# Splitting the attention stage's weight blocks in two halves of 512 columns

## The chip, the core and the metric

The kernel runs on one core of a Trainium2 chip. The metric is the device time of one execution in microseconds (us). TensorE (PE in the profile) multiplies; VectorE (DVE), ScalarE (ACT) and GpSimd (POOL) do elementwise work; SyncE (SP) issues almost all DMA transfers. Each engine works through its own queue in order and waits on semaphores for the others.

## The reference, cut to what matters

One layer of a diffusion backbone, for 1024 latent tokens and 128 context tokens (1152 in all, nine tiles of 128), with a model width of 1024, all in float32:

```
h = rmsnorm(x, g1) * (1 + sc1) + sh1
u_f, q, k, v, g = split(h @ w_in)          # 512 + 1024 + 256 + 256 + 2048 columns
attn_o = attention(rope(q), rope(k), v)    # 16 query heads, 4 kv heads, window +-128, sink
m = sigmoid(g_f) * (fourier_mix(u_f) @ w_fo) + sigmoid(g_a) * (attn_o @ w_ao)
x = x + ga1 * (m @ w_out)
x = x + ga2 * (relu(h2 @ w_ff1) ** 2 @ w_ff2)
y = rmsnorm(x, final_g)
```

The change touches how the columns of `w_in` that make `q` (1024 columns) and the gate logits `g` (2048 columns) are prepared while the attention runs.

## The kernel before, in words

A float32 product is computed as three products of reduced-precision parts. Each operand is split into a high part, `hi = cast(x)` to the type F32R, and a low part, `lo = x - hi`; then `hi*hi + hi*lo + lo*hi` is summed in PSUM (`mm3`, lines 192 to 195). The cast is made on ACT, the subtraction on DVE (`sub`, line 140).

A weight block comes in as 128 partitions x 1024 columns of float32. `load_w` (line 152) takes a raw buffer `wraw` (two of them, shared by every weight load of this stage), issues the load on SP, and calls `split` (line 142), which takes one of three `whi` and one of three `wlo` buffers, casts the whole block on ACT (line 145) and subtracts the whole block on DVE (line 140). The raw buffer is free for the next load when the subtraction has read it.

The attention stage (lines 887 to 925) runs over 36 units: 4 kv groups x 9 token tiles. In a step of the loop, the program emits, in this order: the q projection of the next unit (`attention_q`: 24 matmuls, rotary on DVE, four transposes); the scores of this unit (`attention_scores`: matmuls at L705 and L706, mask and row maximum on DVE at L707, exponentials on ACT at L719, scaling on POOL at L729); the output of the unit before (`attention_out`: transposes at L748, cast `ph` on ACT at L753, subtraction `pl` on DVE, matmuls at L758 and L759, and `ot`/`at` at L762 to L765); and one filler. A filler (`filler`, line 488) is a third of a gate block: 24 matmuls (`gemm_unit`) whose result goes to DRAM. The first filler of a gate block also calls `load_w`. Of the 48 fillers 32 are emitted in this loop, and with them the weight blocks of gates 6 to 15: ten blocks of 8 x 128 columns.

The q weights come in per kv group: `load_q` (line 654) loads two blocks of 4 x 256 columns, k tiles 0 to 3 and 4 to 7, through the same raw buffers, casts each whole (line 662) and subtracts each whole. There are two `qwh` and two `qwl` buffers, so a group's q weights can be written only when the last q projection of the group before has read them. That makes eight blocks. Beside all this, ACT and POOL accumulate a modulation product (L303, L305), with a little DVE work at its end (L321, L322).

The order of the instructions in each engine's queue isn't the order of the program text. The kernel is built with `schedule_with_timeline_sim=True`: a planner simulates the engines, and when an engine comes free it takes, of what is ready in its simulation, what the program emitted first. The queues are then fixed. On the chip an instruction that is late holds up all that stands behind it on its engine.

Of the kernel before, what the change touches and what calls it, by code (L numbers as in the profile page):

```python
# [58 lines left out]
def backbone_kernel(  # L59
# [26 lines left out]
    nc = tc.nc  # L86
    uid = [0]

    def nm(s):
        uid[0] += 1  # L90
        return f"{s}_{uid[0]}"
# [47 lines left out]
    def sub(eng, dst, raw, hi):  # L139
        eng.tensor_tensor(dst, raw, hi.bitcast(F32), ALU.subtract)  # L140

    def split(raw, shape, lo_eng=None):
        hi = wp.tile(shape, F32R, tag="whi", name=nm("whi"), bufs=3)
        lo = wp.tile(shape, F32R, tag="wlo", name=nm("wlo"), bufs=3)
        nc.scalar.copy(hi, raw)  # L145
        sub(lo_eng or nc.vector, lo, raw, hi)
        return hi, lo

    def raw_w(shape):
        return wp.tile(shape, F32, tag="wraw", name=nm("wraw"), bufs=2)  # L150

    def load_w(src, r0, nk, c0, ncol):
        raw = raw_w([P, nk, ncol])
        nc.sync.dma_start(raw, src[r0 * P : (r0 + nk) * P, c0 : c0 + ncol].rearrange("(k p) n -> p k n", p=P))
        return split(raw, [P, nk, ncol])
# [181 lines left out]
    with ExitStack() as sf:  # L337
# [150 lines left out]
        def filler(n, after=None):  # L488
            for _ in range(n):
                if gates:  # L490
                    if after is None:
                        gates.pop(0)()
                    else:
                        with tc.issue_after(after):
                            gates.pop(0)()
# [5 lines left out]
        for o in range(0, NDFT, 1024):  # L501
            n = min(1024, NDFT - o)
            raw = raw_w([P, n])
# [81 lines left out]
    with ExitStack() as s1x:  # L585
# [68 lines left out]
        def load_q(g):  # L654
            out = []
            for hf in range(2):
                raw = raw_w([P, 4, 256])
                c0 = OFF_Q + g * 256
                nc.sync.dma_start(raw, w_in[hf * 512 : (hf + 1) * 512, c0 : c0 + 256].rearrange("(k p) n -> p k n", p=P))
                hi = p1.tile([P, 4, 256], F32R, tag="qwh", name=nm("qwh"), bufs=2)  # L660
                lo = p1.tile([P, 4, 256], F32R, tag="qwl", name=nm("qwl"), bufs=2)
                nc.scalar.copy(hi, raw)
                sub(nc.vector, lo, raw, hi)
                out.append((hi, lo))
            return out

        def attention_q(g, i, qw):
            psq = q1.tile([P, 512], F32, tag="q", name=nm("q"), bufs=1)
            r = slice(i * P, (i + 1) * P)
            for k in range(KC):  # L670
                wh, wl = qw[k // 4]
                mm3(psq[:, :256], h_hi[k][:, r], h_lo[k][:, r], wh[:, k % 4, :], wl[:, k % 4, :], k == 0, k == KC - 1)
            qsrc = psq[:, :256].rearrange("p (h d) -> p h d", h=4)
            qr = p1.tile([P, 4, HD], F32, tag="qr", name=nm("qr"), bufs=2)
            qhl = p1.tile([P, 4, 2, HD], F32R, tag="qhl", name=nm("qhl"), bufs=2)
            if i < 8:
                apply_rope(qr, qsrc, i, qhl[:, :, 0, :])
            else:
                nc.scalar.copy(qr, qsrc)
                nc.scalar.copy(qhl[:, :, 0, :], qsrc)  # L680
            sub(nc.vector, qhl[:, :, 1, :], qr, qhl[:, :, 0, :])
            psT = q1.tile([P, 512], F32R, tag="ptp", name=nm("ptp"), bufs=2)
            for h in range(4):
                ins = nc.tensor.transpose(
                    psT[:, h * P : (h + 1) * P], qhl[:, h].rearrange("p a d -> p (a d)"), identr
                )
            anchor = ins.ins
            qT = p1.tile([P, 4, P], F32R, tag="qT", name=nm("qT"), bufs=2)
            nc.scalar.copy(qT.rearrange("p h t -> p (h t)"), psT)  # L689
            return qT, anchor  # L690
# [80 lines left out]
        def load_kv(g):  # L771
            kd = p1.tile([P, 10, 2, HD], F32, tag="kd", name=nm("kd"), bufs=1)
            for e in range(2):
                nc.sync.dma_start(kd[:, :, e, :], kr_d[:, :, g, :])
            vg = p1.tile([P, 10, 2, HD], F32R, tag="vg", name=nm("vg"), bufs=2)
            nc.gpsimd.dma_start(vg, vh_d[:, :, g])
            return kd, vg

        def put_k(kd, q):
            pk = q1.tile([P, 512], F32, tag="ptp", name=nm("ptp"), bufs=2)  # L780
            for b in range(4):
                kb = {"c": 9, "x": 8}.get(KT_ORDER[q * 4 + b], KT_ORDER[q * 4 + b])
                nc.tensor.transpose(pk[:, b * P : (b + 1) * P], kd[:, kb].rearrange("p a d -> p (a d)"), ident)
            sl_ = slice(q * 512, (q + 1) * 512)
            nc.scalar.copy(kth[:, sl_], pk)
            sub(nc.vector, ktl[:, sl_], pk, kth[:, sl_])
# [5 lines left out]
        def load_fx():  # L792
            wfo.append(load_wfo(0))
            for i in range(4):
                raw = raw_w([P, FC])
                nc.sync.dma_start(raw, f_d[i])
                hi, lo = (slot(2 * i + e)[:, 0:FC] for e in range(2))
                nc.scalar.copy(hi, raw)
                sub(nc.vector, lo, raw, hi)
                fx.append((hi, lo))  # L800
            raw = raw_w([P, FC])
            nc.gpsimd.memset(raw, 0.0)
            for k in range(3):
                for r in range(2):
                    nc.sync.dma_start(raw[32 * k + 2 * r : 32 * k + 2 * r + 2], f_d[2 + r][0:65:64])
            ex, wex = fexw
            nc.scalar.copy(ex, raw[0:96])
            sub(nc.vector, ex[32:36], raw[32:36], ex[32:36])
            raw = raw_w([P, D])
            nc.gpsimd.memset(raw, 0.0)  # L810
            for k in range(3):
                nc.sync.dma_start(raw[32 * k : 32 * k + 4], w_fo.rearrange("(g c) n -> g c n", g=4)[:, 64])
            nc.scalar.copy(wex, raw[0:96])
            sub(nc.vector, wex[64:68], raw[64:68], wex[64:68])
# [69 lines left out]

        fbuf.append(fbuf_p1)

        units = [(g, i) for g in range(NG) for i in range(NTT)]
        kv = {0: load_kv(0)}
        qw = load_q(0)
        for q in range(3):  # L890
            put_k(kv[0][0], q)
        nxt = attention_q(0, 0, qw)
        pending = None
        for s, (g, i) in enumerate(units):
            qT, anchor = nxt
            if s + 1 < len(units):
                g1, i1 = units[s + 1]
                if i1 == 0:
                    qw = load_q(g1)
                nxt = attention_q(g1, i1, qw)  # L900
                anchor = nxt[1]
            pts = attention_scores(g, i, qT)
            if i == 0 and g:
                put_k(kv[g][0], 2)
            if g + 1 < NG:
                if i == 2:
                    kv[g + 1] = load_kv(g + 1)
                if i == 4:
                    put_k(kv[g + 1][0], 0)
                if i == 7:  # L910
                    put_k(kv[g + 1][0], 1)
            if pending is not None:
                attention_out(*pending)
                if s % SKIP:
                    filler(1, anchor)
            pending = (g, i, pts, kv[g][1])
            if s >= len(units) - 2:
                if s == len(units) - 2:
                    filler(100, anchor)
                    load_fx()  # L920
                f_unit(NF)
# [36 lines left out]
    with ExitStack() as sao:  # L958
# [18 lines left out]
        for m in range(KC):  # L977
            if m < 7:
                hi, lo = ER[:, 2 * m * NT : (2 * m + 1) * NT], ER[:, (2 * m + 1) * NT : (2 * m + 2) * NT]
            else:  # L980
                hi, lo = (p3.tile([P, NT], F32R, name=nm("at7")) for _ in range(2))
# [949 lines left out]
```

## Time and profile before

| | |
|---|---|
| time, median of 3 runs | 1698.27 us (1697.79 to 1698.74) |
| profiled execution, its own time | 1695.32 us |
| span of the profiled execution | 1693.5 us |
| PE busy, whole span | 97% |
| DVE, ACT, POOL busy, whole span | 70%, 53%, 18% |
| attention stage | about 228 to 690 us of the span |
| mean granted TensorE clock, whole span | 0.995 |

"Busy" is time in which an instruction of that engine was running. For PE it is time in which at least one matmul was in flight, so it is not the same as full speed. A window's row gives, for each engine, the busy us and the number of instructions, then the granted TensorE clock (1.00 is full speed), the busy share of the DMA engines and their rate. In rows of a timeline the first number is the start, the second the duration, both in us; the square bracket at the end tells how long the engine stood idle before the instruction, and what it waited for.

### The profile page before, as it was taken

The numbers are of one execution on the slowest core, as the hardware profiler recorded it, in microseconds if no ns is written. First come the engines' busy times: TensorE is split into PE (matmuls) and PEld (weight loads), VectorE is DVE, ScalarE is ACT, GpSimd is POOL, SyncE is SP. The second block draws the span as 40 slices with busy tenths as digits, with TensorE's granted clock in tenths as the row PEclk, the third lists the DMA queues.
The fourth block names the chain that finished last, engine by engine and source line by source line (L and its number), as shares of the span: only waits on it lengthen the run. The fifth ranks groups of instructions, "written<-read, shape, count | busy, mean of one in ns | idle before, by whom it ended". The sixth has DMA issues, their size and how long they took to land.

```text
span 1693.5 us, 26361 instructions
## 1 busy us (share of the span) xinstructions
PE 1635.2 (97%) x9053; PEld 1450.9 (86%) x9053; DVE 1184.4 (70%) x2408; ACT 903.8 (53%) x1826; POOL 297.5 (18%) x374
## 2 busy tenths in 40 slices
PE   6999999999999999899999899999999999999997
PEld 5799889999899999889988788888888888888886
DVE  7653247778777877778757876777776488776764
ACT  6443236766767767655436664444444454444542
POOL 3510004435444534400001500000000200000000
PEclk9999999999999999999999999999999999999999
DMA  8342391223322321279656434455446996656751
GB/s 298 114 133 70 128 256 51 77 76 80 90 75 79 94 59 51 78 245 313 197 183 202 156 107 152 159 168 168 161 151 152 307 381 205 199 190 195 244 167 62
DMA packets 204629, 265.56 MB, mean 157 GB/s; under 512 B 31992, under 2 KB 132280, under 8 KB 204496
## 3 DMA queue, kind: packets, MB, share of 16 engines
q1 hardware_dynamic: 196240, 253.92, 46.7%
q0 software_dynamic: 8256, 9.96, 2.3%
q8 instruction: 71, 1.16, 0.3%
q14 instruction: 62, 0.51, 0.1%
HBM read 195.38 MB, written 68.44 MB: 156 GB/s over the span
## 4 chain that ended last, share of the span: by engine, by line
PE 77%; DVE 8%; ACT 4%; issue 3%; DMA 2%; POOL 1%; SPq 0%; DVEq 0%; ACTq 0%; POOLq 0%
PE x L1674 6%; PE x L1675 6%; PE x L1673 6%; PE x L1277 6%; PE x L1279 6%; PE x L1278 6%; PE mm L193 3%; PE mm L194 3%; PE mm L195 3%; PE x L193 2%; PE x L194 2%; PE x L195 2%; PE ptp L748 2%; DVE pt L707 2%; PE o L759 1%
## 5 line engine op out<-in xcount | busy, mean ns | idle before, releaser
L140 DVE TENSOR_TENSOR wlo<-wraw,whi 128x1024 fp32r<-128x1024 f32 x100 | 125.8, 1260 | 80.7 <-ACT whi L145 80.5
L145 ACT CAST whi<-wraw 128x1024 fp32r<-128x1024 f32 x98 | 102.5, 1050 | 90.1 <-PE x L233 20.1
L1674 PE MATMUL x<-BR 128*128 128x512 f32 x336 | 130.7, 389 | 0.0
L1675 PE MATMUL x<-BR 128*128 128x512 f32 x336 | 130.2, 389 | 0.0
L1673 PE MATMUL x<-BR 128*128 128x512 f32 x336 | 129.0, 389 | 0.0
L729 POOL TENSOR_SCALAR pt<-pt,mx 128x512 f32<-128x512 f32 (+2 forms) x144 | 97.2, 687 | 158.1 <-DVE mx L727 141.8
L719 ACT ACTIVATE pt<-pt,mx 128x513 f32<-128x513 f32 (+2 forms) x144 | 94.7, 660 | 33.2 <-DVE mx L717 32.7
L707 DVE CUSTOM_DVE_ANT_0 pt<-s,mask,sink 128x512 f32<-128x512 f32 (+2 forms) x144 | 94.7, 673 | 20.4 <-PE ptp L748 11.3
L1646 ACT CAST BR<-aa 128x512 fp32r<-128x512 f32 x80 | 49.7, 621 | 103.5 <-PE x L1674 48.3
L140 DVE TENSOR_TENSOR pl<-ptp,ph 128x512 fp32r<-128x512 f32 (+1 forms) x136 | 86.0, 640 | 15.9 <-ACT ph L753 14.8
L305 POOL TENSOR_TENSOR macc<-macc,mprod 128x512 f32<-128x512 f32 x70 | 92.2, 1317 | 20.2 <-ACT mprod L303 20.1
L194 PE MATMUL mm<-BR,whi 128*128 128x384 f32 x272 | 91.9, 338 | 0.0
L753 ACT CAST ph<-ptp 128x512 fp32r<-128x512 f32 (+1 forms) x136 | 72.6, 546 | 31.7 <-PE ptp L748 30.3
L1277 PE MATMUL x<-BR,whi 128*128 128x512 f32 (+2 forms) x204 | 79.6, 390 | 4.1 <-ACT ZR L1301 2.8
L193 PE MATMUL mm<-BR,whi 128*128 128x384 f32 x240 | 83.5, 348 | 0.0
L195 PE MATMUL mm<-BR,wlo 128*128 128x384 f32 x240 | 81.2, 338 | 0.0
L748 PE MATMUL ptp<-ident,pt 128*128 128x128 f32 x496 | 76.5, 275 | 2.4 <-ACT qT L689 2.1
L1279 PE MATMUL x<-BR,wlo 128*128 128x512 f32 (+2 forms) x204 | 78.1, 383 | 0.0
L1278 PE MATMUL x<-BR,whi 128*128 128x512 f32 (+2 forms) x204 | 78.0, 382 | 0.0
L303 ACT ACTIVATE mprod<-mraw,siluc 128x256 f32<-128x256 f32 x140 | 63.8, 503 | 20.6 <-POOL macc L305 19.5
L140 DVE TENSOR_TENSOR BR<-aa,BR 128x512 fp32r<-128x512 f32 x80 | 55.0, 687 | 28.3 <-ACT BR L1646 27.7
L1673 PEld LDWEIGHTS x<-BR 128*128 128x128 f32 x336 | 63.1, 188 | 13.2
(462 smaller groups left out, 5199.8 us busy)
## 6 DMA issues: line engine op xcount, KB each, us to landing
aa<-hr_d SPq DMA_DIRECT2D x108, 256.0 KB
ab<-in_w_ff_dram SPq DMA_DIRECT2D x108, 256.0 KB
hr_d<-ZR SPq DMA_DIRECT2D x104, 256.0 KB
wraw<-in_w_in_dram SPq DMA_DIRECT2D x40, 512.0 KB
wraw<-in_w_ff_dram SPq DMA_DIRECT2D x34, 512.0 KB
mraw<-in_w_ada_dram SPq DMA_DIRECT2D x96, 128.0 KB
wraw<-in_w_out_dram SPq DMA_DIRECT2D x24, 512.0 KB
z_d<-z SPq DMA_DIRECT2D x48, 192.0 KB
```

The source lines that it names most:

```text
L140: eng.tensor_tensor(dst, raw, hi.bitcast(F32), ALU.subtract)
L193: nc.tensor.matmul(out, ah, bh, start=start, stop=False)
L194: nc.tensor.matmul(out, ah, bl, start=False, stop=False)
L195: return nc.tensor.matmul(out, al, bh, start=False, stop=stop).ins
L707: nc.vector.tensor_tensor_reduce(out=pt[:, e, :n], in0=sp[:, :n], in1=mask[:, m0 : m0 + n], scale=1.0, scalar=sink8[:, h0 + e : h0 + e + 1 ...
L748: nc.tensor.transpose(pst[:, bi, e, :], pt[:, e, b * P : (b + 1) * P], ident)
L1277: nc.tensor.matmul(po, wh, xh, start=(k == 0 and not cont), stop=False, skip_group_check=cont)
L1278: nc.tensor.matmul(po, wh, xl, start=False, stop=False, skip_group_check=cont)
L1279: nc.tensor.matmul(po, wl, xh, start=False, stop=(k == 3), skip_group_check=cont)
L1673: nc.tensor.matmul(ps, xh, bh, start=start, stop=False, skip_group_check=cont)
L1674: nc.tensor.matmul(ps, xh, bl, start=False, stop=False, skip_group_check=cont)
L1675: nc.tensor.matmul(ps, xl, bh, start=False, stop=stop, skip_group_check=cont)
```

## The change

`split` gets a switch, `parts`. With `parts[0] == 1` it does what it did. While `parts[0]` is 2, it casts and subtracts a block in two halves: cast of half 0, subtraction of half 0, cast of half 1, subtraction of half 1, as the program emits them. The switch is 2 from the start of the attention loop to its last step but one, so it holds for the ten gate blocks; `load_q` does the same for its eight blocks at all times. Each half is 512 columns. Buffers, loads, matmuls and numbers computed stay the same.

```diff
+    parts = [1]
+
     def split(raw, shape, lo_eng=None):
         hi = wp.tile(shape, F32R, tag="whi", name=nm("whi"), bufs=3)
         lo = wp.tile(shape, F32R, tag="wlo", name=nm("wlo"), bufs=3)
-        nc.scalar.copy(hi, raw)
-        sub(lo_eng or nc.vector, lo, raw, hi)
+        if parts[0] == 1:
+            nc.scalar.copy(hi, raw)
+            sub(lo_eng or nc.vector, lo, raw, hi)
+            return hi, lo
+        n = shape[1] // parts[0]
+        for i in range(parts[0]):
+            c = slice(i * n, (i + 1) * n)
+            nc.scalar.copy(hi[:, c], raw[:, c])
+            sub(nc.vector, lo[:, c], raw[:, c], hi[:, c])
         return hi, lo
...
                 hi = p1.tile([P, 4, 256], F32R, tag="qwh", name=nm("qwh"), bufs=2)
                 lo = p1.tile([P, 4, 256], F32R, tag="qwl", name=nm("qwl"), bufs=2)
-                nc.scalar.copy(hi, raw)
-                sub(nc.vector, lo, raw, hi)
+                for c in (slice(0, 2), slice(2, 4)):
+                    nc.scalar.copy(hi[:, c], raw[:, c])
+                    sub(nc.vector, lo[:, c], raw[:, c], hi[:, c])
                 out.append((hi, lo))
...
+        parts[0] = 2
         units = [(g, i) for g in range(NG) for i in range(NTT)]
         kv = {0: load_kv(0)}
         qw = load_q(0)
...
             if s >= len(units) - 2:
+                parts[0] = 1
                 if s == len(units) - 2:
                     filler(100, anchor)
                     load_fx()
```

## The prediction

> **What bounds the kernel now.** I read the page first: the busy shares and the chain of work that ended last.
>
> ```profile
> span 1693.5 us, 26361 instructions
> ...
> PE 1635.2 (97%) x9053; PEld 1450.9 (86%) x9053; DVE 1184.4 (70%) x2408; ACT 903.8 (53%) x1826; POOL 297.5 (18%) x374
> ...
> PE 77%; DVE 8%; ACT 4%; issue 3%; DMA 2%; POOL 1%; SPq 0%; DVEq 0%; ACTq 0%; POOLq 0%
> ```
>
> PE sets the time: busy for 97% of the span and 77% of the chain. So the change counts only where it alters PE's idle time or PE's clock. The profiled execution took 1695.32 us, 1.82 us more than its span; the median shown is 2.95 us above it. I work out a difference on the trace and put it on the median.
>
> Second, the busy time by window: the attention stage (228 to 690), then 3.41 us windows around each stretch in which the clock was halved, and one more window (692) for comparison.
>
> ```profile
> core 0: us, PE busy (x) PEld busy (x) DVE busy (x) ACT busy (x) POOL busy (x), PEclk, DMA share, GB/s
> 371.15:374.56 3.41, 1.62 (x10) 1.17 (x8) 2.86 (x6) 2.46 (x7) 0.55 (x2) 1.00 0.08 22
> 374.56:377.97 3.41, 3.41 (x16) 3.19 (x15) 2.23 (x8) 0.81 (x2) 0.00 (x0) 0.50 0.72 216
> 429.18:432.59 3.41, 1.88 (x12) 1.42 (x11) 3.17 (x10) 3.19 (x8) 1.63 (x3) 1.00 0.51 148
> 432.59:436.00 3.41, 3.41 (x15) 3.41 (x15) 3.08 (x6) 2.30 (x5) 0.00 (x0) 0.50 0.24 60
> 555.47:558.88 3.41, 1.72 (x13) 1.39 (x12) 3.41 (x8) 2.98 (x6) 1.05 (x2) 1.00 0.28 88
> 558.88:562.29 3.41, 3.41 (x13) 2.57 (x13) 3.41 (x8) 0.71 (x2) 0.93 (x2) 0.50 0.75 220
> 692.00:695.41 3.41, 1.77 (x13) 1.44 (x12) 1.71 (x5) 2.43 (x6) 1.59 (x4) 1.00 0.47 176
> ...
> 228.00:690.00 462.00, 443.03 (x3085) 424.79 (x3085) 347.22 (x937) 317.54 (x789) 200.25 (x276) 0.99 0.30 83
> ```
>
> In the stage PE is busy for 443.0 of 462 us, DVE for 75%, ACT for 69%. Three times the clock is granted at 0.50 for 3.41 us while PE is busy throughout; each time the window before had PE busy for half or less (1.62, 1.88, 1.72 us). Each stretch costs 3.41 x 0.5 = 1.7 us, the three 5.1 us. The window at 692 had 1.77 us and kept its clock, so the level near which it falls isn't sharp.
>
> Third, the waits of PE and of its weight loads over the stage (us in total, times, longest).
>
> ```profile
> PE s L705 <- DVE mx L707: 5.8, 8, 1.6
> PE o L759 <- DVE pl L140: 4.0, 3, 1.7
> PE ptp L684 <- DVE pl L140: 3.7, 4, 1.6
> ...
> PEld q L194 <- DVE qwl L140: 0.3, 1, 0.3
> ```
>
> PE waits for DVE's softmax and `pl` results, and but once, for 0.3 us, for a weight split. Splits hurt by standing in front of others, which the timeline shows at four places (DVE rows, then the PE row that waited).
>
> ```profile
> 330.28 1.23 DVE L140 TENSOR_TENSOR wlo<-wraw,whi 128x1024 fp32r<-128x1024 f32 x1 [0.71 <-ACT whi L145]
> 331.42 0.75 DVE L707 CUSTOM_DVE_ANT_0 pt<-s,mask,sink 128x512 f32<-128x512 f32 x1
> ...
> 332.23 0.50 PE L705 MATMUL s<-kth,qT 128*128 128x512 f32 x1 [1.06 <-DVE mx L707]
> ...
> 370.00 1.03 ACT L145 CAST whi<-wraw 128x1024 fp32r<-128x1024 f32 x1
> 371.05 0.26 ACT L762 COPY ot<-o 64x128 f32<-64x128 f32 x1
> ...
> 372.24 1.23 DVE L140 TENSOR_TENSOR wlo<-wraw,whi 128x1024 fp32r<-128x1024 f32 x1
> 373.50 0.62 DVE L707 CUSTOM_DVE_ANT_0 pt<-s,mask,sink 128x384 f32<-128x384 f32 x1
> ...
> 374.18 0.45 PE L705 MATMUL s<-kth,qT 128*128 128x384 f32 x1 [1.47 <-DVE mx L707]
> ...
> 428.17 1.23 DVE L140 TENSOR_TENSOR qwl<-wraw,qwh 128x1024 fp32r<-128x1024 f32 x1 [1.22 <-ACT qwh L662]
> ...
> 430.14 1.07 ACT L753 CAST ph<-ptp 128x512 fp32r<-128x512 f32 x2
> ...
> 431.63 1.28 DVE L140 TENSOR_TENSOR pl<-ptp,ph 128x512 fp32r<-128x512 f32 x2
> ...
> 432.37 0.42 PE L759 MATMUL o<-pl,vg 128*128 128x256 f32 x1 [0.95 <-DVE pl L140]
> ...
> 556.33 1.19 DVE L140 TENSOR_TENSOR wlo<-wraw,whi 128x1024 fp32r<-128x1024 f32 x1
> 557.43 0.41 DVE L322 TENSOR_REDUCE red<-mraw 128x8 f32<-128x256 f32 x1
> 557.75 0.68 DVE L140 TENSOR_TENSOR pl<-ptp,ph 128x512 fp32r<-128x512 f32 x1
> ...
> 558.49 0.39 PE L759 MATMUL o<-pl,vg 128*128 128x256 f32 x1 [1.69 <-DVE pl L140]
> ```
>
> At 330, 372 and 556 a 1.2 us subtraction runs directly or one short step ahead of what PE waits for; near 428 the subtraction is ahead of a queue of softmax work that ends in the wait at 432. Three of the four lie in the windows before a halved clock.
>
> **The change part by part.** Eighteen casts of 1024 columns become 36 of 512, and so the subtractions. No transfer, buffer or matmul changes.
>
> ```profile
> L1646 ACT CAST BR<-aa 128x512 fp32r<-128x512 f32 x80 | 49.7, 621 | 103.5 <-PE x L1674 48.3 <-issue 40.6 <-DMA aa<-hr_d 10.2
> L662 ACT CAST qwh<-wraw 128x1024 fp32r<-128x1024 f32 x8 | 8.4, 1054 | 2.2 <-DMA wraw<-in_w_in_dram 2.2
> L140 DVE TENSOR_TENSOR BR<-aa,BR 128x512 fp32r<-128x512 f32 x80 | 55.0, 687 | 28.3 <-ACT BR L1646 27.7
> ```
>
> *Added work.* A cast of 512 columns from SBUF takes 0.621 us elsewhere in this kernel, a subtraction 0.687 us. Where two halves are parted by other work, a block costs 2 x 0.621 - 1.054 = +0.19 us on ACT and 2 x 0.687 - 1.23 = +0.14 us on DVE. Where they follow each other, they overlap: the two `pl` at 431.63 took 1.28 us together, +0.05, and the two `ph` at 430.14 1.07 us, +0.02. For 18 blocks that is 1.3 us at least, 18 x 0.33 = 5.9 us at most, on both engines together. It is hidden by their idle time in the stage (115 us on DVE, 144 us on ACT); without that cover it would all be PE's loss. The bounds are 0 and +5.9; I take +1.0, the lower sum with most of it on the path, since PE's waits above are for DVE, and DVE's input there comes from ACT.
>
> [...]
>
> *Work let in between.* If the planner puts a waiting instruction between the halves, it starts 1.23 - 0.687 = 0.54 us sooner behind a subtraction, 1.05 - 0.62 = 0.43 us behind a cast (at 371.05 `ot` stands right behind a 1.03 us cast, and `at` on DVE behind it). At the four places that is 4 x 0.54 + 0.43 = 2.6 us at most. The order is fixed by simulated times, so the slot may go to an instruction that nobody waits for. I take half, -1.3; bounds -2.6 and 0.
>
> *The clock.* With 0.54 us more of PE work, the three windows would hold 2.2 to 2.4 us, above all three that led to a halved clock. I take two of three gone: -3.4; bounds -5.1 and, since a re-planned order can stall PE elsewhere, +3.4 (two new stretches).
>
> *An earlier first half.* The second q block of group 1 is read as soon as it is there:
>
> ```profile
> 334.38 1.18 DVE L140 TENSOR_TENSOR qwl<-wraw,qwh 128x1024 fp32r<-128x1024 f32 x1
> ...
> 335.62 0.39 PE L194 MATMUL q<-qwl,BR 128*128 128x256 f32 x1
> ```
>
> PE reads it 0.06 us after its end. Two of its four k tiles would be there 0.54 us sooner, but score matmuls fill most of that wait: 0 to -0.5, I take -0.3. For the other blocks the 0.3 us of direct waits above is the cap, so they earn nothing.
>
> *Sum:* +1.0 - 1.3 - 3.4 - 0.3 = -4.0 us. 1695.32 becomes 1691.3 for the profiled execution; on the median, 1698.27 - 4.0 = 1694.3 us.
>
> **The rivals.**
>
> *Nothing moves.* The planner sees both halves ready one behind the other and takes them so; the waiting work stays behind 1.28 us instead of 1.23. For it: a cast's second half needs only the raw block, which is already there. Against it: DVE gets the second half only when ACT has cast it, about half a microsecond after the first (half of the 1.07 us of the two `ph`), time enough for another instruction. The clock stretches stay, the overhead of about 1 us stays: 1699.3 us. [...]
>
> *Everything goes.* All three stretches and all of the waiting in front of splits vanish: +0.6 - 2.6 - 5.1 - 0.5 = -7.6, 1690.7 us. Against it: the planner doesn't know which stall costs a clock stretch.
>
> *Slower: a late second half at a group's head.* Once a subtraction is two instructions, other DVE work can come ahead of the second. At the head of group 1 there is no cover (0.06 us), and behind the q matmul in PE's in-order queue stand scores, outputs and fillers. An L707 (0.75) and a `pl` (0.68) between the halves hold PE for 1.4 us; with the clock stretch such a wait can bring that is 1.4 + 1.7 = 3.1 us. It decides from about one such wait with no relief elsewhere: 1.0 + 3.1 = +4.1, 1702.4 us. For it: DVE is at 75% and three engines hand work round. Against it: only one of the three later heads is that tight in the waits above.
>
> **How the numbers follow.** The forecast has 0.42, with a range of its own from 1691.5 to 1697; everything goes 0.12; nothing moves 0.27; slower 0.19. The limits of a difference that this measurement can tell are 0.2%, 3.4 us: 1694.9 and 1701.7. Of the forecast's chance 0.32 lies below 1694.9 and 0.10 within; all of "everything goes" is below; nothing moves gives 0.24 within and 0.03 above; the slower case 0.16 above and 0.03 within. That is 0.44 faster, 0.37 the same, 0.19 slower. The range reaches to 1688 (everything goes, and some other stalls with it) and to 1702.5 (the slower case).
>
> **What would show it.** Right: on DVE an L707, `pl` or `at` between two halves of 0.69 us; fewer than three windows at clock 0.50 between 228 and 690; PE's waits for L707 and `pl` shorter in sum than 13.5 us. Wrong: halves side by side at all 18 blocks; as many halved stretches, at other places; a PE wait for `qwl` of over 1 us; or a stage whose length changes while its clock stretches don't, which would put the gain or loss in the re-planned order and not in what I summed.

## The result and the profile after

| | before | after |
|---|---|---|
| time, median of 5 runs | 1697.79 us (1695.16 to 1698.74) | 1705.63 us (1704.57 to 1706.86) |
| ratio | | 1.0052, 95% interval 1.0039 to 1.0065 |
| profiled execution, its own time | 1695.32 us | 1704.57 us |
| span of the profiled execution | 1693.5 us | 1702.8 us |
| mean granted TensorE clock | 0.995 | 0.992 |

The change makes the kernel slower by 8.8 us by the ratio (7.8 us between the medians). Its 1705.63 us lie above the forecast of 1694.3 us and above the top of its range, 1702.5 us. The busy shares and the chain hardly show it. They answer the first lines of the prediction:

```profile
span 1702.8 us, 26393 instructions
...
PE 1640.8 (96%) x9053; PEld 1454.9 (85%) x9053; DVE 1187.8 (70%) x2426; ACT 905.8 (53%) x1844; POOL 293.7 (17%) x374
...
PE 76%; DVE 8%; ACT 4%; DMA 3%; issue 2%; POOL 1%; SPq 0%; DVEq 0%; ACTq 0%; POOLq 0%
```

VectorE has 18 instructions and 3.4 us more, TensorE the same 9053 and 5.6 us more. To find the place I took one event that each unit of the attention has once, ScalarE's cast of the transposed q (L689 before, L699 after), and compared its start in both traces. Up to unit 28 the two stay together: 617.31 us before, 618.83 after. At unit 33 they stand at 675.39 and 685.91. So of the 9.3 us by which the spans differ, 1.5 lie ahead of unit 28, nine arise between these two events, and 1.2 us are won back in the 1000 us behind them. The nine are no chance of one execution: in all runs below that keep before's order there, this step takes 58.06 to 58.10 us. Here is that stretch, by window: first from unit 28 to 29, then from 29 to 30, then the whole from 28 to 33. The columns are those of the prediction's windows. Before:

```profile
617.31:626.43 9.12, 9.12 (x63) 8.83 (x63) 7.92 (x21) 7.03 (x19) 4.06 (x6) 1.00 0.24 74
626.43:638.33 11.90, 9.91 (x71) 8.44 (x70) 10.64 (x32) 9.41 (x26) 7.51 (x11) 1.00 0.20 51
617.31:675.39 58.08, 56.09 (x389) 52.98 (x389) 47.78 (x133) 44.86 (x116) 28.17 (x39) 1.00 0.19 58
```

and after:

```profile
618.83:631.92 13.09, 11.17 (x78) 10.61 (x77) 11.89 (x37) 9.54 (x26) 6.37 (x9) 1.00 0.28 83
631.92:644.83 12.91, 11.06 (x66) 9.82 (x67) 11.04 (x28) 9.20 (x25) 8.04 (x11) 0.87 0.08 22
618.83:685.91 67.08, 60.50 (x394) 56.44 (x393) 49.99 (x141) 45.36 (x118) 29.97 (x41) 0.95 0.17 51
```

The whole stretch is 67.08 us instead of 58.08, nine more. TensorE stands idle for 67.08 - 60.50 = 6.6 us of it, where it was 58.08 - 56.09 = 2.0: 4.6 us of new waits. It is busy for 4.4 us longer, and the granted clock of 0.95 says why: two half-clock stretches lie in it, which cost 2 x 3.41 x 0.5 = 3.4 us. The last 1.0 us goes with the five more matmul records that fall into this window. The stretches show in aligned windows, each with the window ahead of it:

```profile
628.97:632.38 3.41, 1.48 (x13) 1.22 (x11) 3.33 (x13) 2.76 (x8) 1.13 (x3) 1.00 0.45 132
632.38:635.79 3.41, 3.41 (x12) 2.61 (x11) 3.35 (x7) 2.65 (x9) 2.16 (x3) 0.50 0.07 19
656.27:659.68 3.41, 1.54 (x11) 1.37 (x12) 2.90 (x10) 2.13 (x5) 2.32 (x3) 1.00 0.07 19
659.68:663.09 3.41, 3.41 (x13) 3.41 (x11) 1.91 (x6) 1.74 (x5) 1.33 (x2) 0.50 0.13 38
```

**No halved block is anywhere near.** The last one of the changed kernel is subtracted at 584 us; the one weight block of this stretch, at 624 us, is split whole in both kernels. What differs is the order. From 624 us in the changed kernel, on VectorE and on TensorE (start, duration, and in the bracket the idle time and what ended it):

```profile
624.43 1.35 DVE L140 TENSOR_TENSOR wlo<-wraw,whi 128x1024 fp32r<-128x1024 f32 x1 [0.97 <-PE mm L204]
...
629.54 0.46 PE L694 MATMUL ptp<-identr,qhl 128*128 128x128 f32 x4
631.94 1.31 PE L758 MATMUL ptp<-ident,pt 128*128 128x128 f32 x6 [1.94 <-DVE pl L140]
...
629.49 0.75 DVE L717 CUSTOM_DVE_ANT_0 pt<-s,mask,sink 128x512 f32<-128x512 f32 x1
630.17 0.75 DVE L717 CUSTOM_DVE_ANT_0 pt<-s,mask,sink 128x512 f32<-128x512 f32 x1
631.37 0.42 DVE L140 TENSOR_TENSOR pl<-ptp,ph 128x256 fp32r<-128x256 f32 x1
```

and the same transposes of unit 29 before:

```profile
625.40 0.46 PE L684 MATMUL ptp<-identr,qhl 128*128 128x128 f32 x4
...
626.35 0.28 PE L193 MATMUL q<-qwh,BT 128*128 128x256 f32 x1
...
627.77 0.28 PE L195 MATMUL q<-qwh,BR 128*128 128x256 f32 x1
627.89 0.82 PE L748 MATMUL ptp<-ident,pt 128*128 128x128 f32 x6
```

Before, ten matmuls of a q projection, which depend on nothing in the softmax, and four score matmuls stand between the transposes of q and the next transposes of probabilities. After, all 24 of that projection have been issued ahead, the `pl` that PE waits for stands on VectorE behind two softmax passes of 0.75 us, and PE waits 1.94 us. Whether the missing matmuls or the order on VectorE make this wait, these rows can't say.

The places that the prediction named look like this in the changed kernel:

```profile
330.20 0.69 DVE L140 TENSOR_TENSOR wlo<-wraw,whi 128x512 fp32r<-128x512 f32 x1
330.81 0.75 DVE L717 CUSTOM_DVE_ANT_0 pt<-s,mask,sink 128x512 f32<-128x512 f32 x1
...
332.15 1.34 DVE L140 TENSOR_TENSOR wlo<-wraw,whi 128x512 fp32r<-128x512 f32 x1
...
373.67 1.29 DVE L140 TENSOR_TENSOR wlo<-wraw,whi 128x512 fp32r<-128x512 f32 x2
...
375.67 0.44 PE L715 MATMUL s<-kth,qT 128*128 128x384 f32 x1 [1.54 <-DVE mx L717]
...
547.16 2.51 DVE L140 TENSOR_TENSOR qwl<-wraw,qwh 128x512 fp32r<-128x512 f32 x4
...
552.26 0.51 PE L694 MATMUL ptp<-identr,qhl 128*128 128x128 f32 x4 [2.39 <-DVE pl L140]
```

At 330 two softmax passes come between the halves as forecast, and the wait of 1.06 us there is gone. At 372 the halves lie side by side (1.29 us for both), and the wait is 1.54 us where it was 1.47. The wait at 556 has given way to a worse one at 552: two q blocks, four halves in a row, then 2.39 us. Over the stage, 228 to 700 us, PE's waits (us in total, times, longest):

```profile
PE ptp L694 <- DVE pl L140: 9.7, 9, 2.4
PE o L768 <- DVE at L775: 4.2, 4, 1.6
PE s L715 <- DVE mx L717: 3.0, 4, 1.5
PE ptp L758 <- DVE pl L140: 2.3, 2, 1.9
PE o L769 <- DVE pl L140: 2.1, 3, 0.9
```

Waits for the row maximum fell from 5.8 to 3.0 us; waits for `pl` rose from 4.0 + 3.7 to 9.7 + 2.3 + 2.1, and those for `at` from 1.3 to 4.2.

### The profile page after: what moved, and what is told of

Read it like the earlier page. It is cut to its first block, busy times and chain, and to the rows that moved or that the text cites. A ratio compares the mean times of both kernels' runs of the same rounds, so it can differ in the third digit from the quotient of the medians.

```text
span 1702.8 us, 26393 instructions
## 1 busy us (share of the span) xinstructions
PE 1640.8 (96%) x9053; PEld 1454.9 (85%) x9053; DVE 1187.8 (70%) x2426; ACT 905.8 (53%) x1844; POOL 293.7 (17%) x374
## 4 chain that ended last, share of the span: by engine, by line
PE 76%; DVE 8%; ACT 4%; DMA 3%; issue 2%; POOL 1%; SPq 0%; DVEq 0%; ACTq 0%; POOLq 0%
PE x L1686 6%; PE x L1687 6%; PE x L1685 6%; PE x L1289 6%; PE x L1291 6%; PE x L1290 6%; PE mm L202 3%; PE mm L203 3%; PE mm L204 3%; PE x L202 2%; PE x L203 2%; PE x L204 2%; PE ptp L758 2%; DVE pt L717 2%; PE x L240 1%
## 5 line engine op out<-in xcount | busy, mean ns | idle before, releaser
L140 DVE TENSOR_TENSOR wlo<-wraw,whi 128x1024 fp32r<-128x1024 f32 (+1 forms) x110 | 130.8, 1194 | 82.6 <-ACT whi L148 73.0
L148 ACT CAST whi<-wraw 128x1024 fp32r<-128x1024 f32 x88 | 92.1, 1051 | 84.4 <-PE x L242 21.8
L729 ACT ACTIVATE pt<-pt,mx 128x513 f32<-128x513 f32 (+2 forms) x144 | 94.8, 662 | 36.4 <-DVE mx L727 35.9
L1686 PEld LDWEIGHTS x<-BR 128*128 128x128 f32 x336 | 63.1, 188 | 13.1
L1685 PEld LDWEIGHTS x<-BR 128*128 128x128 f32 x336 | 63.0, 188 | 13.1
```

The source lines that it names most:

```text
L1685: nc.tensor.matmul(ps, xh, bh, start=start, stop=False, skip_group_check=cont)
L1686: nc.tensor.matmul(ps, xh, bl, start=False, stop=False, skip_group_check=cont)
```

## The experiments

The planner writes the order anew for every program. Set side by side in queue order, at least 581 TensorE, 218 VectorE, 119 ScalarE and 53 SyncE instructions stand elsewhere in the changed kernel. To part order from halves I fixed the order by hand: after the program is emitted, an order-only edge joins each instruction of a queue to the next, in an order read from another kernel.

```diff
         backbone_kernel(tc, *args)
+        pin(tc, second)
...
+        for a, b in zip(queue, queue[1:]):
+            tc.add_manual_dep(b, a.name, info, reason="pin")
```

A second half, where the order comes from a kernel with whole blocks, stands right behind its first. All kernels below compute everything. "Step" is the time from unit 28's cast of the transposed q to unit 33's in the profiled execution.

| run | blocks | order | ratio to before | interval | step, us |
|---|---|---|---|---|---|
| before | whole | own | 1 | | 58.08 |
| the change | 18 halved | own | 1.0052 | 1.0039 to 1.0065 | 67.08 |
| order_before_halves | 18 halved | before's | 1.0000 | 0.9991 to 1.0008 | 58.07 |
| order_after_whole | whole | the change's | 1.0042 | 1.0029 to 1.0055 | 67.06 |
| halves_q_only | 8 q blocks halved | own | 1.0068 | 1.0056 to 1.0080 | 68.92 |
| halves_gate_only | 10 gate blocks halved | own | 1.0037 | 1.0020 to 1.0053 | 68.23 |
| late_order_after | whole | before's, the change's from 612 us | 1.0058 | 1.0043 to 1.0073 | 68.05 |
| early_order_after | whole | the change's, before's from 612 us | 1.0003 | 0.9992 to 1.0015 | 58.10 |
| one_solid_projection | whole | before's, one edit | 1.0011 | 1.0000 to 1.0022 | 58.95 |
| second_halves_behind | 18 halved | before's, three edits | 1.0014 | 1.0003 to 1.0025 | 58.06 |
| one_late_block | 1 halved | own | 1.0057 | 1.0041 to 1.0073 | 67.17 |
| one_early_block | 1 halved | own | 0.9980 | 0.9968 to 0.9993 | 58.06 |
| late_order_first_part | whole | the change's from 612 to 640 us | 1.0026 | 1.0015 to 1.0036 | 62.81 |
| late_order_second_part | whole | the change's from 640 us | 1.0049 | 1.0034 to 1.0063 | 66.58 |
| early_block_order_whole | whole | one_early_block's | 0.9981 | 0.9967 to 0.9994 | 58.07 |
| early_block_order_halves | 18 halved | one_early_block's | 0.9984 | 0.9972 to 0.9995 | 58.06 |
| second_part_act_moved | whole | second part, one edit | 1.0035 | 1.0023 to 1.0048 | 64.72 |
| second_part_act_last | whole | second part, one edit | 1.0032 | 1.0019 to 1.0045 | 64.11 |
| late_order_act_moved | whole | late order, one edit | 1.0056 | 1.0043 to 1.0070 | 67.56 |
| late_order_act_last | whole | late order, one edit | 1.0039 | 1.0024 to 1.0054 | 65.58 |

### Is it the order, or the halves?

Three theories stood at the start: P, the loss is the re-planned order; W, the halves cost it by their instructions; G, late second halves at the heads of groups stall PE. The first run has the change's halves in before's order, the second before's whole blocks in the change's order.

> The 36 halves of the change, but every engine's queue fixed in the order that the kernel before has, each second half right behind its first. Theory P (the loss is the re-planned order of the queues): within 0 to +1.5 us of before, the added instructions' price where two halves follow each other (18 x 0.05 to 0.07 us on DVE). Theory W (the halves themselves cost it, by their added instructions): +6 to +9 us, as the change. Theory G (a late second half at a group's head stalls PE): 0 to +1.5, since no second half is late here.

> Whole blocks as before, but every engine's queue fixed in the order that the changed kernel has (a whole cast or subtraction stands where its first half stood). Theory P: +6 to +10 us against before, as the change. Theory W: within 1.5 us of before. Theory G: within 1.5 us of before, since no second half exists.

Measured: 1695.85 us, level with before, and 1702.99 us, 0.42% over it. The step of each, in the window columns:

```profile
620.00:678.07 58.07, 56.10 (x389) 53.03 (x389) 47.77 (x133) 44.88 (x115) 28.15 (x39) 1.00 0.20 58
```

```profile
615.86:682.92 67.06, 60.27 (x394) 56.64 (x393) 49.95 (x141) 45.33 (x118) 29.90 (x41) 0.95 0.17 51
```

The first window is that of the halves in before's order, the second that of whole blocks in the change's order. P holds, W and G fall: halves without the order cost nothing that can be measured, and the order without halves costs the same nine microseconds in the same step. Fixing the order costs nothing that shows either: here with halves, and in `early_order_after` below with whole blocks.

Next, each part of the change alone, the planner free to order.

```diff
-        parts[0] = 2
+        parts[0] = 1
```

```diff
-                for c in (slice(0, 2), slice(2, 4)):
+                for c in (slice(0, 4),):
```

> Only the eight q blocks in halves, the planner free. Theory P: a third order, with a time of its own between -5 and +10 us that is not a share of the change's loss. Theory W: 8 of 18 blocks, +3.5 us. Theory G: all of the loss, +6 to +9 us.

> Only the ten gate blocks in halves, the planner free. Theory P: a fourth order, between -5 and +10 us; with the q blocks' run it need not add up to the change. Theory W: 10 of 18 blocks, +4.3 us. Theory G: within 1 us of before.

Measured: 1.0068 and 1.0037 (1707.54 and 1702.76 us). Each part alone loses about as much as both together, in steps of 68.92 and 68.23 us. The q blocks alone lose 11.5 us (9.5 to 13.6), above the 10 us that P had allowed. The parts don't add up, which a cost per block would do.

### Which part of the order?

Whole blocks again. One kernel takes before's order up to about 612 us, after the last of the 18 blocks, and the change's from there; the other is its mirror image.

> Whole blocks, as before. All queues in before's order up to the last of the 18 blocks (about 612 us of the span), from there in the changed kernel's order. Theory T (the loss comes from the re-planned order of units 28 to 33, where no block is split): the step from the transposed q of unit 28 to that of unit 33 is 9 to 11 us longer than before's, the time is 6 to 10 us over before, and half-clock stretches lie near 630, 657 and 705. Theory E (the loss is sown earlier, and the late order is only fitted to it): within 2 us of before.

> Whole blocks, as before. All queues in the changed kernel's order up to about 612 us of the span, from there in before's order. Theory T: between 2 us under before and 1.5 us over it, and the step from unit 28 to unit 33 as long as before's, within 1 us. Theory E: 6 to 10 us over before.

Measured: 1707.11 us, 1.0058; and 1697.33 us, 1.0003. The late order alone is the whole loss; the early one, in which all 18 blocks lie, is level with before.

Then the late order was cut in two at 640 us, the transposes of unit 30.

> Whole blocks, before's order in all queues but from about 612 to 640 us of the span, where the changed kernel's order stands (to the transposes of unit 30). If each badly placed stretch of the order costs what its own wait and clock stretch take: 5 to 7 us over before, +5 to +6 at the transposed q of unit 30 and nothing more behind it. If the loss is one thing that runs through the whole late order: near 0 or near 10.

> Whole blocks, before's order in all queues up to about 640 us of the span (the transposes of unit 30), from there the changed kernel's. By the reading that each stretch costs its own: 2 to 5 us over before, with a TensorE wait of 1.7 + 1.2 us for the output of unit 29 and a half-clock stretch behind it. If the loss needs the first part: within 1 us of before.

Measured: 1.0026, some 4.4 us (2.5 to 6.1), and 1.0049, 8.3 us (5.8 to 10.7). The first part is a little under the 5 to 7 us expected; its step is 4.7 us longer than before's. The second loses more than the 2 to 5 us expected. In time, 4.4 + 8.3 can't be told from the 9.8 us (7.3 to 12.4) of the whole late order; in the steps, 4.7 + 8.5 stand against 10.0. So a bad stretch of order does cost its own, but the parts are not independent: behind before's first part, the second part's wait for the output of unit 29 is 3.17 us long; in the changed kernel it was 1.51.

One edit was tried that looked like the mechanism of the first wait: in before's order, only unit 32's 24 matmuls of the q projection moved into one block, as the change has them.

> Whole blocks, before's order in all queues but for one edit: in TensorE's queue the 24 matmuls of unit 32's q projection, which before's order spreads over 36 places among the output matmuls, transposes and scores of units 26 to 28, stand in one block ahead of the output of unit 26, as the changed kernel's order has them. Theory S (the dependent instructions lost the independent matmuls between them, and TensorE now waits for the softmax on VectorE and ScalarE): 1.5 to 4 us over before, lost between the transposed q of units 28 and 30. If other moves of the late order are the cause: within 1 us of before.

Measured: 1.0011, 1.9 us at a point, interval 0 to 3.7, which decides nothing; the step is 0.9 us longer. Between units 28 and 29:

```profile
617.60:627.91 10.31, 10.31 (x72) 9.98 (x72) 8.28 (x22) 7.04 (x20) 4.05 (x6) 1.00 0.30 91
```

These 1.2 us more than before hold nine more matmuls and no wait; 0.3 us come back by unit 30. The first wait of the changed kernel, 1.94 us at 631.94, isn't there at all: between units 28 and 30, PE waits for 2.2 us, where before it waited for 2.0. So the lost cover on PE doesn't make that wait alone. VectorE's order, in which two softmax passes stand ahead of the `pl`, is the next suspect, and no run tests it.

### One block is enough

The order of the queues can be read from a program without running it. With one single block in halves, 11 of the 18 choices leave before's order all but unchanged (at most 19 instructions moved on any engine), and 7 move from 130 to 259 TensorE instructions. Two of these were run: the eighth gate block, which brings the change's late order, and the third, which re-plans only the units ahead of it.

```diff
-        if parts[0] == 1:
+        calls[0] += inatt[0]
+        if not (inatt[0] and calls[0] in (8,)):
```

> One block of the eighteen in halves, the eighth of the ten gate blocks; all others whole, and the planner free to order. It moves at least 259 TensorE and 113 VectorE instructions against before's order, and from the transposes of unit 28 on TensorE's queue stands as in the changed kernel. Theory T (the late order is the loss): 6 to 11 us over before, 8.5 to 11 of it between the transposed q of units 28 and 33, though no block is split there. If the loss needs many halves: within 1 us of before.

> One block of the eighteen in halves, the third of the ten gate blocks; all others whole, and the planner free to order. It moves at least 176 TensorE and 79 VectorE instructions against before's order, but between units 27 and 33 TensorE's queue stands as before. Theory T: within 2 us of before, the step from unit 28 to unit 33 as long as before's within 1 us. If any re-planned order costs some 0.5%: 6 to 10 us over.

Measured: 1706.72 us, 1.0057, and 1694.19 us, 0.9980 (0.9968 to 0.9993). In the first kernel the block is split in two at 504 us, and nine microseconds are lost more than 100 us later:

```profile
504.37 0.69 DVE L140 TENSOR_TENSOR wlo<-wraw,whi 128x512 fp32r<-128x512 f32 x1
...
616.44:683.61 67.17, 60.26 (x394) 56.63 (x393) 50.00 (x141) 45.38 (x117) 29.98 (x41) 0.95 0.17 51
```

The second, as much edited, is 0.2% faster than before, so it beats both kernels. That is a miss of the expectation in the good direction: "within 2 us" was expected, 3.4 us came (1.2 to 5.4). To tell whether the order or the half block gains, its order was given to whole blocks and to all eighteen in halves.

> Whole blocks, all queues in the order that the planner made for the kernel with one early block in halves. If the order is what gains there: 2 to 5 us under before, and 2 to 4 us of it between the transposed q of units 0 and 28. If the halves of the one block gain: within 1 us of before.

> All eighteen blocks in halves, as in the changed kernel, and all queues in the order of the kernel with one early block in halves (each second half right behind its first). If order sets the time and halves are free: 2 to 5 us under before, within 1.5 us of the whole blocks in the same order. If halves cost the 1.0 us that the prediction summed for added work: 1 us over the whole blocks in the same order, which these rounds can hardly tell.

Measured: 0.9981 and 0.9984 (1694.22 and 1695.46 us). The order gains, and again the halves add nothing that can be told. Where it gains stays open. The expectation put it between units 0 and 28, which take 359.27 us before and 358.02 and 355.55 us in these two; but nine executions in before's order up to 612 us or further, before's own among them, spread from 356.44 to 361.08 us there.

### The prediction's own mechanism, made by hand

The prediction counted on waiting instructions getting in between two halves. In before's order with halves, three second halves on VectorE were moved behind the instruction that PE waits for. All three are of gate blocks (`wlo`), though the expectation calls them q blocks.

> Halves at all 18 blocks, all queues in before's order, but the VectorE second halves of three q blocks are moved behind the instruction that TensorE waits for (at 330 and 372 behind the copy of the transposed quarters, L707 of before, at 556 behind the probabilities pl). It does by hand what the prediction counted on. By the prediction's mechanism: TensorE's waits of 1.06, 1.47 and 1.69 us there are each some 0.5 us shorter, the half-clock stretches at 374 and 558 are gone, and the time is 1.5 to 5 us under before. If the stretches do not hang on these waits: the waits shorter, the stretches there, and the time within 1.5 us of before. If TensorE then waits for the second half itself: not under before.

Measured: 1.0014 (1.0003 to 1.0025): not faster, but some 2 us slower. The place at 372 tells why it isn't faster. With the halves side by side:

```profile
373.73 1.29 DVE L140 TENSOR_TENSOR wlo<-wraw,whi 128x512 fp32r<-128x512 f32 x2
375.60 0.69 DVE L140 TENSOR_TENSOR pl<-ptp,ph 128x512 fp32r<-128x512 f32 x1
...
375.74 0.44 PE L721 MATMUL s<-kth,qT 128*128 128x384 f32 x1 [1.54 <-DVE mx L723]
```

With the softmax between them:

```profile
374.44 0.62 DVE L723 CUSTOM_DVE_ANT_0 pt<-s,mask,sink 128x384 f32<-128x384 f32 x1
374.98 0.69 DVE L140 TENSOR_TENSOR wlo<-wraw,whi 128x512 fp32r<-128x512 f32 x1
375.59 0.68 DVE L140 TENSOR_TENSOR pl<-ptp,ph 128x512 fp32r<-128x512 f32 x1
...
375.12 0.44 PE L721 MATMUL s<-kth,qT 128*128 128x384 f32 x1 [0.93 <-DVE mx L723]
...
376.33 0.38 PE L775 MATMUL o<-pl,vg 128*128 128x256 f32 x1 [0.59 <-DVE pl L140]
```

The wait is 0.61 us shorter, as forecast, and 0.59 us of it come back at the next matmul, which waits for a `pl` that starts at 375.59 instead of 375.60. VectorE has as much to do up to there as before. At the other two places it is alike: at 330 a wait of 0.61 us goes and one of 0.60 us comes, behind ScalarE's `qhl`; at 556 the wait falls from 1.66 to 1.06 us, and the next score matmul waits 0.41 us. The clock does as little: of this kernel's aligned windows,

```profile
375.07:378.49 3.42, 2.78 (x19) 2.46 (x20) 3.14 (x9) 0.96 (x4) 0.19 (x1) 1.00 0.32 82
...
560.08:563.49 3.41, 1.93 (x8) 1.03 (x8) 3.41 (x9) 0.59 (x1) 0.98 (x2) 1.00 0.76 226
563.49:566.90 3.41, 3.41 (x17) 3.41 (x16) 1.61 (x5) 2.92 (x7) 0.25 (x2) 0.50 0.25 70
```

the one at 375 keeps its clock, the stretch near 558 has only moved to 563, and a new one lies at 700, where before had none. Where the 2 us are lost, this trace, of an execution of 1696.98 us, doesn't show.

### What makes the second part's wait

In the second part's trace ScalarE waits 3.70 us for the weights of a modulation block, and the exponentials (L729) stand behind that step in its queue; VectorE's next reciprocal waits for them, and PE for an output freed behind that.

```profile
648.82 0.91 ACT L312 ACTIVATE macc<-mraw,siluc 128x256 f32<-128x256 f32 x2 [3.70 <-DMA mraw<-in_w_ada_dram]
650.27 0.91 ACT L312 ACTIVATE mprod<-mraw,siluc 128x256 f32<-128x256 f32 x2 [0.54 <-DMA mraw<-in_w_ada_dram]
651.09 0.71 ACT L729 ACTIVATE pt<-pt,mx 128x513 f32<-128x513 f32 x1
...
654.10 0.36 PE L768 MATMUL o<-ph,vg 128*128 128x256 f32 x1 [3.17 <-DVE at L775]
655.40 0.58 PE L769 MATMUL o<-pl,vg 128*128 128x256 f32 x1 [0.95 <-DVE pl L140]
```

Four ScalarE instructions were moved back in its queue, first behind the exponentials and output copies, then behind the casts `ph` too, each in the second part and in the whole late order. The ten instructions concerned, in queue order, by the tile that they write:

```diff
-ACT: macc macc mprod mprod pt pt ot ot ph ph
+ACT: pt pt ot ot macc macc mprod mprod ph ph
...
+ACT: pt pt ot ot ph ph macc macc mprod mprod
```

> As the second part of the late order, but on ScalarE the first two products of one modulation block (four instructions of 0.5 us that wait for their weights, near 649 us) stand behind the two exponentials and the two output copies of unit 29 and not ahead of them. If ScalarE's in-order queue makes TensorE's wait: the exponentials start with their row maximum, 1.3 us sooner, the wait of 3.2 us for the output of unit 29 falls to 2 us or less, the half-clock stretch of 6.8 us behind it to 3.4 or none, and the time to 2 to 5 us over before, against 8. If VectorE's order makes it: the wait and the time stay, within 1 us.

> As the whole late order, with the same four instructions of ScalarE moved behind the output copies of unit 29. If ScalarE's queue makes the wait near 655 us (1.5 + 0.95 us in the changed kernel): 1.3 to 4 us less than the whole late order, so 6 to 8.5 us over before. If VectorE's order makes it: as the whole late order, within 1 us.

Measured: 1.0035, 5.9 us over before and just outside the 2 to 5 us expected. The first wait is still 3.24 us, now for `ph` behind the moved instructions, where 2 us or less was expected; the second is 0.34 us. In the whole late order 1.0056, 9.5 us, no change that can be told, where 6 to 8.5 us were expected. So the casts were moved ahead as well.

> As the second part of the late order, the four modulation instructions of ScalarE behind the two exponentials, the two output copies and the two casts ph of unit 29's second pair. If ScalarE's queue is the cause: the wait of 3.2 us falls by the 1.7 us that these four take, to about 1.5 us, and the time to 1 to 3.5 us over before. If VectorE's order is the next limit: the wait stays over 2.5 us and the time near 4.7 us over.

> The same move in the whole late order. If ScalarE's queue is the cause of the wait near 655 us: that wait, 1.64 us with the first move, falls to 0.5 us or less, and the time to 5 to 8 us over before, since the waits near 630 and 641 us stay. If VectorE's order is the next limit: as the whole late order, 9 to 10 us over.

Measured: 1.0032, 5.4 us over before, where 1 to 3.5 us were expected, and 1.0039, 6.6 us, within the 5 to 8 us expected. In the second part:

```profile
653.90 0.35 PE L768 MATMUL o<-ph,vg 128*128 128x256 f32 x1 [1.92 <-DVE at L775]
655.20 0.39 PE L769 MATMUL o<-pl,vg 128*128 128x256 f32 x1 [0.95 <-DVE pl L140]
```

The wait fell from 3.17 to 1.92 us, 1.25 of the 1.7 expected, and in the late order the wait at that place falls from 1.59 to 0.63 us. So ScalarE's in-order queue behind a late transfer makes about 1.3 us of the second part's waits of 3.17 + 0.95 = 4.1 us. The intervals of the times (1.0049 against 1.0032, 1.0058 against 1.0039) overlap, so in time the effect is likely, not shown. What holds the remaining 2.9 us, VectorE's order by its bracket, was not taken apart.

## Why the prediction was wrong

**The step that failed** is the frame of the sum: it put a price on what happens at the 18 blocks and put the re-planned order of everything else at nothing, but for a bound on the clock. The order of units 28 to 33, behind the last halved block, was written anew, and this step became 9 us longer. The runs showed in its place a loss of 7 to 10 us that whole blocks in that order have too (1.0042 and 1.0058), while all 18 blocks in halves at a fixed order cost 0.0 us. That bound, two new stretches or +3.4 us, was the only harm of re-planning that the prediction allowed. It named the true case in its last part, a gain or loss "in the re-planned order and not in what I summed", and gave it neither a term nor a chance; its slower rival had another mechanism, and PE's waits for `qwl` stayed at 0.8 us in all.

**Added work**, +1.0 us, bounds 0 to +5.9. At a fixed order halves cost 0.0 us (-1.5 to +1.4), and 0.5 us at a point in the second pair. Two halves side by side take 1.29 us on VectorE where one block took 1.23: the small overlap price was right, and none of it reaches the time. Parted by a softmax pass, as by hand at 372, they take 0.69 us each, 0.15 us more than the block; neighbours take 0.06 us more.

**Work let in between**, -1.3 us. Right in size at the wait: 0.61 us by hand, against 0.54 forecast. Wrong in what it is worth: at 372 the next wait took 0.59 us of it. The prediction asked what starts sooner and not what is late next. Its reading that PE waits for the softmax and for `pl` also left out the waits for `at`, 1.3 us before and 4.2 after. Also half right on where: on ScalarE all 18 pairs lie side by side, on VectorE nine are parted, among them 330, but not 372 and 428.

**The clock**, -3.4 us, was the largest term and the least founded. In the change's stage from 228 to 690 us there are four stretches, at 376, 554, 632 and 660 us, where three were; with the waits cut by hand a stretch vanished and others came. In before's own order with halves side by side the stage has two, at 376 and 434, and none near 558, where PE waits 1.66 us as before. The term read three stretches of a single execution as properties of three waits.

**An earlier first half**, -0.3 us: no sign of it. PE waits 0.8 us for `qwl` in the stage; before, only its weight loads did, for 0.3 us.

**The rivals.** "Nothing moves" was right about 372 and 428 and about the price of the halves, and wrong in its name: order moved everywhere. "Everything goes" and "a late second half" did not come; the +0.6 for added work in the sum of the former has no row behind it. The kernel did get slower, to which the prediction gave 0.19, but not by the mechanism that it gave for it.

## What to carry to other kernels

In a kernel whose queues come from a planner, an edit's own cost and the cost of the new order are two quantities; measure the first with the old order held fixed. The second can be the larger: here 0.0 us against -3 to +12 us, for edits of one block to all 18. Before summing savings, compare the new queue orders with the old ones, also far from the edit, and look which loads an in-order queue now waits for (1.3 us here). That independent matmuls no longer stand ahead of a wait is worth a look too, but here it did not make the wait alone. And a wait that is cut is worth only what the next wait on the same engine leaves: at 372 a wait 0.61 us shorter, and 0.59 us of new wait behind it.

## What the runs showed of the hardware

**Half-clock stretches lie on a grid of 3.413 us.** In each profiled execution they start whole multiples of 3.413 us apart: before, 374.56, 432.59 and 558.88 are 17 and 37 steps apart. Against the start of the span the grid stands elsewhere in each of the 20 traces, by 0.3 to 3.35 us. What went ahead of them was a window of the grid with little work on PE. Over the 20 traces, from 40 to 1000 us and for windows at full clock, I counted which windows were followed by a halved one: all 45 with up to 1.45 us busy, 59 of 114 with 1.45 to 1.95 us, 3 of 43 with 1.95 to 2.15 us, none of 88 with 2.15 to 2.55 us. So I estimate from these counts that a wait of 2 us that falls into one window, and leaves 3.4 - 2 = 1.4 us of work there, costs a further 3.41 x 0.5 = 1.7 us; cut in equal parts by the grid, it leaves 2.4 us in each of two windows and costs nothing further. Between 1.45 and 1.95 us the busy time doesn't decide it. The wait at 432, in the same order as before, costs no clock in the second part's execution:

```profile
429.40:432.81 3.41, 1.91 (x12) 1.41 (x10) 3.16 (x10) 3.35 (x8) 1.91 (x3) 1.00 0.43 124
432.81:436.23 3.42, 3.36 (x22) 3.36 (x23) 3.28 (x6) 2.36 (x5) 0.00 (x0) 1.00 0.26 72
```

where before had 1.88 us of work in its window and 0.50 behind it. In 29 runs of before on one chip the granted clock went from 0.989 to 0.995 and the time from 1692.25 to 1700.86 us, with a correlation of -0.73; a thousandth of the clock is 1.7 us. So the profiled execution before, at 0.995, was one with few stretches, and about half of the spread of this kernel's times goes with the clock (0.73 squared is 0.53).

**A wait that lost its first releaser had the next one behind it.** The same two groups of matmuls (L768, L769) waited 3.17 + 0.95 us, 3.24 + 0.34 us and 1.92 + 0.95 us in three orders of ten ScalarE instructions: taking away the first releaser showed the next, with all of the first wait still there, and only when both were out of the way did 1.25 us of it go.
